# Hybrid decoder layer, down projection of the MLP: one 1024-column VectorE add per product in place of two 512-column sums shared with ScalarE and GpSimd, a new order of the products, and a smaller GpSimd share in the MLP

## The chip, the core and the metric

One core of one Trainium2 chip runs the whole layer. The metric is the device time of one execution in microseconds; three runs of the kernel before give a median of 2394.18 us (2391.11 to 2404.26). Engines are named as in the profile: PE (TensorE matmul), PEld (its weight loads), DVE (VectorE), ACT (ScalarE), POOL (GpSimd), SP (the engine that issues the DMAs).

## The reference

A decoder layer on 2048 tokens of width 1024: a mixer (two groups of gated linear attention heads) and an MLP, each between two RMSNorms. The change lies in the MLP, and almost all of it in the second product:

```python
h = x + rmsnorm(hybrid_mixer(rmsnorm(x, pre_mix_norm), ...), post_mix_norm)
u = jnp.square(jax.nn.relu(rmsnorm(h, pre_mlp_norm) @ w_up))   # 2048x1024 @ 1024x4096
out = h + rmsnorm(u @ w_down, post_mlp_norm)                   # 2048x4096 @ 4096x1024
```

All is float32, and the kernel keeps float32 accuracy.

## The kernel before

The layer runs as three stages one after the other: the mixer (matmuls on lines 232 to 234), `up` (962 to 964) and `down` (1192 to 1194). In this kernel each float32 operand of a matmul is split into a high part of type fp32r and a rest of the same type, `hi` and `lo`, and a product takes three matmuls: hi by hi, hi by lo, lo by hi. The split is `parts()`: ACT copies `raw` to `hi` (L859), and then a subtraction `lo = raw - hi` goes through `tt()`, which gives it to POOL (L850) or DVE (L853). `tt()` keeps a running load for both engines and takes POOL while POOL's sum plus 1.36 is below DVE's plus 0.85. A second layer `_x`, computed without these splits, stands behind a condition and is not executed; all names here end in `_f`.

The MLP's matmuls use a form of Strassen's scheme (Winograd's): a block of 2 x 2 needs seven products, numbered 0 to 6, in place of eight, and sums and differences around them. In `down`, `w_down` is taken in 8 blocks of 512 rows (`kb`). A block has four granules `n` (`GRAN`: 256 tokens of each half block of tokens), and each granule seven products of 12 matmuls: 336 matmuls in a block, 2688 in all. Product `i` of granule `n` reads `u[n, i]` (the activations, combined in `up`, stored in DRAM as `u_operands`, tiles `raw_f` and `u_f`) and `wd[kb][i]` (split weights in the tiles `act_f`). The weights come as four DMAs of 512 KB into the tiles `wr_f` (`down_weights`, L1049); their four differences (tiles `t_f` and `wr_f`) and 14 splits of 512 columns are done in the seven steps ahead of the block's first product and on into its first granule. A step is one product.

Each product adds into one of three PSUM banks, by token half `x`: X holds products 0 and 1, Y 5, 6 and 3, Z 4 and 2, accumulating one on the other. After each product its bank is added into an SBUF tile `acc_f`, and the next product on that bank must wait until the bank is read (and the first of the next granule until a buffer is free: 3 X, 3 Y, 2 Z, each 128 x 512). Those sums are of two kinds:

- `grow()`: DVE adds the bank directly, `acc += bank` (L1131);
- `later()`, for products 5 and 6: ACT copies the bank to a tile `y_f` (L1157), then POOL adds `acc += y` (L1135).

In the first block ACT copies the bank into `acc_f` instead. In the last block the sums of products 5 and 6 also take the sum `a` of product 0 along (DVE `y = bank + acc a`, then an addition by `tt`), and `c21 += a` is a further `tt`. Each finished quarter is squared on ACT with a row sum (L1172) and multiplied with the gain `post` by `tt`; when both halves of a row are there, `finish()` forms the reciprocal root (L239 on DVE, the power L241 on POOL), applies it and adds the residual (L1263 on DVE) and stores the rows (L1266). The residual rows are loaded at L1168, on SP's queue, like the `u` inputs of `down_input` (L1093; one product per DMA, issued seven steps ahead, split five steps ahead).

The order in the program is set by the list `todo` of `down`, sorted by step; on top of it a scheduler reorders the finished program statically for each engine, so the same code elsewhere in the layer can come out in a slightly different order when tiles change.

Of the kernel before, what the change touches and what calls it, by code (L numbers as in the profile page):

```python
# [96 lines left out]
class Layer:  # L97
# [72 lines left out]
    def aslot(self):  # L170
        return self.ac.tile([P, TB], F32R, tag="act", name=self.name("act"), bufs=32)
# [194 lines left out]
    def prepare(self, b, ahead=1):  # L366
# [149 lines left out]
    def tile_task(self, u, i, q, k, g, scale):  # L516
# [31 lines left out]
        for h, og in outs:  # L548
# [4 lines left out]
            self.oT[n] = self.split(self.aslot(), self.aslot(), tr, self.normw[:, n:n + 1])  # L553
# [283 lines left out]
    def left(self, s, i, raws, out, slot):  # L837

        for j in range(4):
# [3 lines left out]
            out.append(self.parts(slot, raw))  # L843

    def tt(self, out, a, b, op):

        nc = self.nc
        if self.load[1] + 1.36 < self.load[0] + 0.85:
            self.load[1] += 1.36
            nc.gpsimd.tensor_tensor(out, a, b, op)  # L850
        else:
            self.load[0] += 0.85
            nc.vector.tensor_tensor(out, a, b, op)  # L853

    def parts(self, new, raw, shape=None):
        hi, lo = new(), new()
        if shape is not None:
            hi, lo = (z.rearrange("p (k n) -> p k n", k=shape) for z in (hi, lo))
        self.nc.scalar.activation(hi, raw, AF.Copy)  # L859
        self.tt(lo, raw, hi.bitcast(F32), ALU.subtract)  # L860
# [15 lines left out]
    def up(self):  # L876
# [3 lines left out]
        with ExitStack() as ctx:  # L880
# [13 lines left out]
            def slot():  # L894


                return self.aslot() if self.place else new("a", 24, F32R)

            def left(s, i):
# [4 lines left out]
                for _ in self.left(s, i, lambda: new("raw", 3), ops[s, i], slot):  # L904
                    pass

            def right(n):
# [11 lines left out]
                part = lambda z: self.parts(lambda: new("w", 12, F32R), z, 4)  # L919
# [121 lines left out]
            self.first_down(lambda: new("wr", 4, F32, 1024), lambda: new("t", 5), lambda: new("raw", 3))  # L1041

    def down_weights(self, kb, wide, temp):
# [3 lines left out]
        for f, h in ((0, 0), (0, 1), (1, 1), (1, 0)):  # L1047
            r = wide().rearrange("p (k n) -> p k n", k=2)
            self.nc.sync.dma_start(r, view[f][:, :, h * 512:h * 512 + 512])  # L1049
            raw.append([r[:, k, :] for k in range(2)])  # L1050
        b11, b12, b22, b21 = raw
        ks = range(2)
        w = self.wd[kb] = {}

        def keep(i, z):
            w[i] = [self.parts(self.aslot, z[k]) for k in ks]

        def diff(out, x, y):
# [19 lines left out]
        keep(4, t1)  # L1078
# [3 lines left out]
        keep(2, b22)  # L1082
        yield


    GRAN = tuple((s, q) for s in range(2) for q in range(2))

    def down_input(self, n, i, raws, slot):

        kb, (s, q) = n // 4, self.GRAN[n % 4]  # L1090
        raw = raws()
        view = self.ud[i, s, 2 * kb:2 * kb + 2].rearrange("k p t -> p k t")
        self.nc.sync.dma_start(raw.rearrange("p (k t) -> p k t", k=2), view[:, :, q * 256:q * 256 + 256])  # L1093
        yield
        self.u[n, i] = self.parts(slot, raw)
        yield

    def first_down(self, wide, temp, raws):

        self.wd, self.u = {}, {}  # L1100
        for _ in self.down_weights(0, wide, temp):
            pass
        for i in self.ORDER[:2]:
            for _ in self.down_input(0, i, raws, self.aslot):
                pass

    def down(self):
# [3 lines left out]
        with ExitStack() as ctx:  # L1111
# [9 lines left out]
            def temp():  # L1121
                return new("t", 4)

            nkb = FF // 512
            npair = 8
            acc, rows = {}, {}
            self.load = [0.0, 0.0]

            def dve_add(out, a, b):
                self.load[0] += 0.69  # L1130
                nc.vector.tensor_add(out, a, b)  # L1131

            def pool_add(out, a, b):
                self.load[1] += 1.36
                nc.gpsimd.tensor_add(out, a, b)  # L1135

            def grow(p, key, z, first):

                if first:
                    acc[p, key] = new("acc", 5 * npair)  # L1140
                    nc.scalar.activation(acc[p, key], z, AF.Copy)
                else:
                    dve_add(acc[p, key], acc[p, key], z)

            def later(p, key, z, first, last):


                if first:
                    acc[p, key] = new("acc", 5 * npair)
                    nc.scalar.activation(acc[p, key], z, AF.Copy)  # L1150
                else:
                    y = new("y", 3)
                    if last:
                        dve_add(y, z, acc[p, "a"])
                        self.tt(acc[p, key], acc[p, key], y, ALU.add)
                    else:
                        nc.scalar.activation(y, z, AF.Copy)  # L1157
                        pool_add(acc[p, key], acc[p, key], y)

            def closed(n, p, key):  # L1160
# [3 lines left out]
                t0 = s * TM + m * TB + q * 256 + p % 2 * P  # L1164
                a = acc[p, key]
                if (p, m) not in rows:
                    h1, ss = wide(), new("ssm", 8, F32, 2)
                    nc.sync.dma_start(h1, self.h1d[t0:t0 + P, :])  # L1168
                    rows[p, m] = (h1, ss, {})
                h1, ss, parts = rows[p, m]  # L1170
                parts[half] = a
                nc.scalar.activation(new("y", 3), a, AF.Square, accum_out=ss[:, half:half + 1])  # L1172
                self.tt(a, a, self.post[half], ALU.mult)
                if len(parts) == 2:
                    tails.append(self.finish(t0, h1, ss, parts))

            def product(n, i):

                kb = n // 4
                hi, lo = (z.rearrange("p (k t) -> p k t", k=2) for z in self.u.pop((n, i)))  # L1180
                b = self.BANK[i]
                for x in range(2):
                    p = 2 * (n % 4) + x
                    first = (p, b) not in bank
                    if first:
                        bank[p, b] = ps.tile([P, TB], F32, tag=b, name=self.name(b), bufs=2 if b == "Z" else 3)
                    z = bank[p, b]
                    tok = slice(x * P, x * P + P)
                    mm = nc.tensor.matmul
# [166 lines left out]
```

## Time and profile before

| what | value |
| --- | --- |
| median of three runs | 2394.18 us (2391.11 to 2404.26) |
| profiled execution, its own time | 2393.46 us |
| its span | 2391.2 us |
| mixer | 0 to 1036.3 us |
| up | 1036.3 to 1702.3 us |
| down, eight blocks | 1702.3 to 2374.3 us |
| after the last matmul | 2374.3 to 2391.2 us |

The stages are told apart by the line of the matmuls. The rows quoted below come from the page, from windows (a stretch, its length, the busy time and count of each engine, then the granted TensorE clock, the DMA share and GB/s), from the waits (engine, tile and line, what it waited for: total, times, longest), from groups (line, engine, operation, out<-in, count | busy us, mean ns | idle time just before them, and what ended it), and from the timeline (start, duration, instruction, [idle before <- what ended it]).

### The profile page before, as it was taken

How to read it: one execution, taken by the hardware profiler on the slowest of the kernel's cores; microseconds unless marked ns; L12 is line 12 of the kernel's file. 1: busy time of each engine (PE TensorE's matmuls, PEld its weight loads, DVE VectorE, ACT ScalarE, POOL GpSimd, SP SyncE). 2: the span in 40 equal slices, each digit the busy share in tenths (PEclk: the TensorE clock that was granted, in tenths of full speed). 3: DMA queues.
4: the chain of work that ended last, by engine and by line, in shares of the span. 5: the costliest groups of instructions: out<-in, count | busy, mean ns of one | idle time of the engine just before them, and what ended most of it. 6: DMA issues, size and time to landing. Idle time of an engine off the chain costs nothing. (4 is left out here: it accounts for less than half of the span.)

```text
span 2391.2 us, 32759 instructions
## 1 busy us (share of the span) xinstructions
PE 2271.7 (95%) x10922; PEld 1852.0 (77%) x10922; DVE 1499.0 (63%) x2492; ACT 1245.3 (52%) x2547; POOL 1156.1 (48%) x855
## 2 busy tenths in 40 slices
PE   7999999999999989979999999999799999999994
PEld 6788878888887878767788878888687777877873
DVE  4675566656755487475545665545556677677698
ACT  5754566456655656455545564554563444334441
POOL 4320323133312542057655665555455677567686
PEclk9999999999999999999999999999899999999997
DMA  6421642256215932278644564444433333333355
GB/s 181 122 79 61 198 133 71 89 147 189 72 57 178 280 113 76 97 240 269 218 153 146 188 214 151 148 146 154 155 110 124 123 123 113 113 119 120 119 169 189
DMA packets 294915, 343.49 MB, mean 144 GB/s; under 512 B 25792, under 2 KB 214480, under 8 KB 294736
## 3 DMA queue, kind: packets, MB, share of 16 engines
q1 hardware_dynamic: 294736, 341.30, 44.8%
q8 instruction: 88, 1.44, 0.2%
q14 instruction: 91, 0.75, 0.1%
HBM read 242.65 MB, written 98.57 MB: 143 GB/s over the span
## 5 line engine op out<-in xcount | busy, mean ns | idle before, releaser
L223 POOL TENSOR_TENSOR w_f<-wr_f,w_f 128x512 fp32r<-128x512 f32 (+1 forms) x160 | 218.8, 1379 | 264.9 <-ACT w_f L222 240.3
L232 PE MATMUL zp_f<-w_f,act_f 128*128 128x512 f32 (+2 forms) x896 | 331.5, 371 | 0.5 <-ACT w_f L222 0.5
L233 PE MATMUL zp_f<-w_f,act_f 128*128 128x512 f32 (+2 forms) x896 | 327.6, 366 | 1.3 <-POOL w_f L223 1.0
L234 PE MATMUL zp_f<-w_f,act_f 128*128 128x512 f32 (+2 forms) x896 | 326.0, 366 | 0.0
L241 POOL TENSOR_TENSOR rs_f<-ms_f,c_neghalf 128x1 f32<-128x1 f32 (+1 forms) x96 | 77.2, 812 | 426.8 <-DVE ms_f L239 426.3
L859 ACT ACTIVATE u_f<-raw_f 128x512 fp32r<-128x512 f32 x222 | 139.4, 630 | 249.7 <-DMA raw_f<-u_operands 65.2
L222 ACT ACTIVATE w_f<-wr_f 128x512 fp32r<-128x512 f32 (+1 forms) x288 | 178.5, 630 | 142.9 <-DMA wr_f<-in_w_in 64.0
L850 POOL TENSOR_TENSOR u_f<-raw_f,u_f 128x512 fp32r<-128x512 f32 x116 | 167.0, 1445 | 99.7 <-ACT u_f L859 80.5
L232 PEld LDWEIGHTS zp_f<-w_f,act_f 128*128 128x128 f32 x896 | 169.4, 189 | 29.9 <-issue 2.2
L233 PEld LDWEIGHTS zp_f<-w_f,act_f 128*128 128x128 f32 x896 | 169.7, 190 | 29.2 <-POOL w_f L223 1.2
L234 PEld LDWEIGHTS zp_f<-w_f,act_f 128*128 128x128 f32 x896 | 169.6, 189 | 27.4 <-issue 0.2
L1135 POOL TENSOR_TENSOR acc_f<-acc_f,y_f 128x512 f32<-128x512 f32 x96 | 141.9, 1482 | 83.8 <-ACT y_f L1157 83.6
L1192 PE MATMUL Y_f<-act_f,u_f 128*128 128x512 f32 x380 | 151.8, 400 | 22.7 <-DVE y_f L1131 13.1
L232 PE MATMUL zp_f<-act_f,w_f 128*128 128x512 f32 x384 | 154.6, 406 | 2.7 <-ACT act_f L222 2.7
L233 PE MATMUL zp_f<-act_f,w_f 128*128 128x512 f32 x384 | 154.7, 403 | 2.1 <-DVE act_f L223 2.1
L853 DVE TENSOR_TENSOR u_f<-raw_f,u_f 128x512 fp32r<-128x512 f32 x106 | 105.1, 992 | 78.8 <-ACT u_f L859 78.8
L234 PE MATMUL zp_f<-act_f,w_f 128*128 128x512 f32 x384 | 153.3, 399 | 0.0
L1193 PE MATMUL Y_f<-act_f,u_f 128*128 128x512 f32 x380 | 150.8, 397 | 0.0
L1194 PE MATMUL Y_f<-act_f,u_f 128*128 128x512 f32 x380 | 149.4, 395 | 0.0
L223 DVE TENSOR_TENSOR w_f<-wr_f,w_f 128x512 fp32r<-128x512 f32 (+1 forms) x128 | 97.7, 775 | 79.0 <-ACT w_f L222 76.7
L859 ACT ACTIVATE w_f<-t_f 128x512 fp32r<-128x512 f32 x128 | 80.0, 628 | 114.8 <-PE Y_f L963 61.4
L850 POOL TENSOR_TENSOR ev_f<-ev_f,ev_f 128x512 f32<-128x512 f32 x67 | 101.5, 1515 | 64.0 <-ACT ev_f L981 63.7
(247 smaller groups left out, 6214.4 us busy)
## 6 DMA issues: line engine op xcount, KB each, us to landing
u_operands<-ev_f SPq DMA_DIRECT2D x224, 256.0 KB, 2.1
raw_f<-u_operands SPq DMA_DIRECT2D x224, 256.0 KB, 2.7
wr_f<-in_w_in SPq DMA_DIRECT2D x256, 128.0 KB, 2.6
wr_f<-in_w_up SPq DMA_DIRECT2D x64, 512.0 KB, 3.7
wr_f<-in_w_in SPq DMA_DIRECT2D x96, 256.0 KB, 3.1
wide_f<-in_x SPq DMA_DIRECT2D x32, 512.0 KB, 6.0
wr_f<-in_w_out SPq DMA_DIRECT2D x64, 256.0 KB, 3.0
wr_f<-in_w_down SPq DMA_DIRECT2D x32, 512.0 KB, 3.7
```

Source lines behind the costliest of these rows:

```text
L222: nc.scalar.activation(hi, raw, AF.Copy)
L223: eng.tensor_sub(lo, raw, hi.bitcast(F32))
L232: mm(out, a[0], b[0], start=i == 0, stop=False)
L233: mm(out, a[0], b[1], start=False, stop=False)
L234: mm(out, a[1], b[0], start=False, stop=i == n - 1)
L850: nc.gpsimd.tensor_tensor(out, a, b, op)
L853: nc.vector.tensor_tensor(out, a, b, op)
L859: self.nc.scalar.activation(hi, raw, AF.Copy)
L1135: nc.gpsimd.tensor_add(out, a, b)
L1192: mm(z, hi[:, k, tok], whi, start=first and k == 0, stop=False, skip_group_check=not first)
L1193: mm(z, hi[:, k, tok], wlo, start=False, stop=False, skip_group_check=not first)
L1194: mm(z, lo[:, k, tok], whi, start=False, stop=k == 1, skip_group_check=not first)
```

## The change

- `down`: every sum after a product is one DVE add of 1024 columns, both token halves at once, directly from PSUM (L1145); only for the last granule's products 2 and 3 it is split in two. There are no copies to `y_f` and no sums on POOL. The banks become tiles of 128 x 1024: X 1, Y 2, Z 1.
- The products' order in `down` is 0, 4, 5, 1, 6, 2, 3 in place of 0, 5, 1, 6, 4, 3, 2. In the last block ACT writes `a` into Y's bank ahead of product 5 (four times, 1024 columns), in place of the extra additions of `a`.
- Inputs of two products are handled together: two DMAs, one copy and one subtraction of 1024 columns; loaded eight steps ahead and split four ahead. The weights' splits and differences are of 1024 columns too (7 and 4 a block); the differences are formed in the `wr_f` tiles themselves.
- `tt()` takes POOL only while POOL's load is below `share` times DVE's; `share` is 0.5, in the last block 1.0 for three granules and 0.5 for the last. This holds in `up` as well.
- The `act_f` tiles are allocated in pairs (also in the mixer and in `up`). `post` is loaded as one tile and scaled by the root of 1024, `finish()` uses one DVE operation ahead of the power in place of two.

```diff
-        if self.load[1] + 1.36 < self.load[0] + 0.85:
-            self.load[1] += 1.36
+        dve, pool = 0.2 + n / 960, 0.1 + n / 400
+        if self.load[1] + pool < self.share * (self.load[0] + dve):
+            self.load[1] += pool
             nc.gpsimd.tensor_tensor(out, a, b, op)
...
+    DOWN = (0, 4, 5, 1, 6, 2, 3)
...
         def keep(i, z):
-            w[i] = [self.parts(self.aslot, z[k]) for k in ks]
+            hi, lo = self.parts(self.along(), self.along(), z, 1024)
+            w[i] = [(hi[:, k * 512:k * 512 + 512], lo[:, k * 512:k * 512 + 512]) for k in range(2)]
...
-        self.u[n, i] = self.parts(slot, raw)
+        hi, lo = self.parts(*pair(), raw, 1024)
+        for x in range(2):
+            self.u[self.seq[m + x]] = [z[:, x * 512:x * 512 + 512].rearrange("p (k t) -> p k t", k=2)
+                                       for z in (hi, lo)]
...
-                        nc.scalar.activation(y, z, AF.Copy)
-                        pool_add(acc[p, key], acc[p, key], y)
...
+                a = acc[p, key]
+                for x in ((slice(0, 512), slice(512, 1024)) if split else (slice(0, 1024),)):
+                    self.load[0] += 1.25
+                    nc.vector.tensor_add(a[:, x], a[:, x], z[:, x])
...
-                        bank[p, b] = ps.tile([P, TB], F32, tag=b, name=self.name(b), bufs=2 if b == "Z" else 3)
+                    bank[n, b] = ps.tile([P, 2 * TB], F32, tag=b, name=self.name(b), bufs=2 if b == "Y" else 1)
...
+                if end and i == 5:
+                    nc.scalar.activation(z, acc[n % 4, "a"], AF.Copy)
+                    loaded = True
...
-                        todo.append((at - 7, 0, "load", n, i))
-                        todo.append((at - 5, 1, "input", n, i))
+                    todo.append((m - 8, 0, "load", m))
+                    todo.append((m - 4, 1, "input", m))
...
-        nc.vector.tensor_add(tot, ss[:, 0:1], ss[:, 1:2])
-        r = self.rstd(tot, D, 1)
+        nc.vector.tensor_scalar(tot, ss[:, 0:1], ss[:, 1:2], D * EPS, ALU.add, ALU.add)
+        r = self.t([P, 1], "rs", bufs=8)
+        nc.gpsimd.tensor_tensor(r, tot, self.c["neghalf"][:, :1], ALU.pow)
```

Two places show how the instructions come to stand. The first is a change of weights: while the last granule of block 4 and the first of block 5 are multiplied, the weights of block 5 are prepared. DVE's queue there, before (L853 on `act_f`, `t_f`, `wr_f` is weight work, L853 on `u_f` the inputs, L1131 the sums from the banks):

```order
L853 TENSOR_TENSOR act_f_19797<-t_f_19792,act_f_19796 128x512
L1131 TENSOR_TENSOR acc_f_16978<-acc_f_16978,X_f_19740 128x512
L1131 TENSOR_TENSOR acc_f_16934<-acc_f_16934,Y_f_19610 128x512
L1131 TENSOR_TENSOR acc_f_16837<-acc_f_16837,Z_f_19670 128x512
L1131 TENSOR_TENSOR acc_f_16846<-acc_f_16846,Z_f_19678 128x512
L853 TENSOR_TENSOR t_f_19793<-wr_f_19576,t_f_19793 128x512
L853 TENSOR_TENSOR act_f_19825<-wr_f_19576,act_f_19824 128x512
L853 TENSOR_TENSOR u_f_19789<-raw_f_19726,u_f_19788 128x512
L853 TENSOR_TENSOR act_f_19829<-wr_f_19576,act_f_19828 128x512
```

and DVE's queue at the same change of weights now:

```order
L1145 TENSOR_TENSOR acc_f_16729<-acc_f_16729,X_f_18777 128x1024
L1145 TENSOR_TENSOR acc_f_16756<-acc_f_16756,Z_f_18803 128x1024
L861 TENSOR_TENSOR wr_f_18654<-wr_f_18658,wr_f_18654 128x1024
L1145 TENSOR_TENSOR acc_f_16714<-acc_f_16714,Y_f_18697 128x1024
L1145 TENSOR_TENSOR acc_f_16776<-acc_f_16776,Y_f_18822 128x1024
L861 TENSOR_TENSOR u_f_18840<-raw_f_18757,u_f_18839 128x1024
L861 TENSOR_TENSOR act_f_18862<-wr_f_18660,act_f_18861 128x1024
L1145 TENSOR_TENSOR acc_f_16802<-acc_f_16802,X_f_18777 128x1024
L861 TENSOR_TENSOR wr_f_18654<-wr_f_18660,wr_f_18654 128x1024
L861 TENSOR_TENSOR act_f_18887<-wr_f_18656,act_f_18886 128x1024
```

A 1024-column sum of every product (Y included) stands between the subtractions, one or two of them at a time. POOL's queue at this place, before:

```order
L850 TENSOR_TENSOR u_f_19709<-raw_f_19664,u_f_19708 128x512
L850 TENSOR_TENSOR t_f_19792<-wr_f_19576,t_f_19792 128x512
L850 TENSOR_TENSOR act_f_19801<-t_f_19793,act_f_19800 128x512
L850 TENSOR_TENSOR u_f_19729<-raw_f_19686,u_f_19728 128x512
L850 TENSOR_TENSOR u_f_19751<-raw_f_19706,u_f_19750 128x512
L1135 TENSOR_TENSOR acc_f_17005<-acc_f_17005,y_f_19773 128x512
L1135 TENSOR_TENSOR acc_f_17014<-acc_f_17014,y_f_19783 128x512
```

and POOL's queue there now:

```order
L858 TENSOR_TENSOR u_f_18728<-raw_f_18647,u_f_18727 128x1024
L858 TENSOR_TENSOR act_f_18818<-wr_f_18654,act_f_18817 128x1024
L858 TENSOR_TENSOR u_f_18795<-raw_f_18724,u_f_18794 128x1024
L858 TENSOR_TENSOR act_f_18844<-wr_f_18654,act_f_18843 128x1024
L858 TENSOR_TENSOR u_f_18882<-raw_f_18791,u_f_18881 128x1024
```

POOL keeps some of the subtractions, now of 1024 columns, and none of the sums. The second place is the last block, DVE's queue before:

```order
L1131 TENSOR_TENSOR acc_f_16822<-acc_f_16822,X_f_21810 128x512
L853 TENSOR_TENSOR acc_f_16726<-acc_f_16726,y_f_21669 128x512
L1131 TENSOR_TENSOR acc_f_16718<-acc_f_16718,Z_f_21678 128x512
L853 TENSOR_TENSOR u_f_21737<-raw_f_21672,u_f_21736 128x512
L1131 TENSOR_TENSOR acc_f_16726<-acc_f_16726,Z_f_21692 128x512
L1131 TENSOR_TENSOR acc_f_16762<-acc_f_16762,Y_f_21596 128x512
L853 TENSOR_TENSOR acc_f_16718<-acc_f_16718,t_f_21355 128x512
```

and DVE's queue in the last block now (L1241 is the former L1263):

```order
L1145 TENSOR_TENSOR acc_f_16511<-acc_f_16511,Y_f_20181 128x1024
L1241 SCALAR_TENSOR_TENSOR acc_f_16369<-acc_f_16369,rs_f_20132,wr_f_20057 128x512
L1241 SCALAR_TENSOR_TENSOR acc_f_16459<-acc_f_16459,rs_f_20132,wr_f_20057 128x512
L1145 TENSOR_TENSOR acc_f_16532<-acc_f_16532,X_f_20142 128x1024
L1241 SCALAR_TENSOR_TENSOR acc_f_16369<-acc_f_16369,rs_f_20138,wr_f_20063 128x512
L1241 SCALAR_TENSOR_TENSOR acc_f_16459<-acc_f_16459,rs_f_20138,wr_f_20063 128x512
L1145 TENSOR_TENSOR acc_f_16511<-acc_f_16511,Z_f_20167 128x1024
L1145 TENSOR_TENSOR acc_f_16496<-acc_f_16496,Y_f_20181 128x1024
L861 TENSOR_TENSOR u_f_20257<-raw_f_20156,u_f_20256 128x1024
```

The additions of `y_f` are gone; sums from the banks and the closing operations are what is left, with an input's subtraction between. The order of a granule's products on PE comes out as 0, 4, the previous granule's 3, then 5, 1, 2, 6.

More of the change, by code (lines that the diff above doesn't have):

```diff
@@ L116, in __init__ @@
         self.load = [0.0, 0.0]
+        self.share = 0.5
         self.tasks = []
@@ L835, in combine, with left @@
             yield
-    def left(self, s, i, raws, out, slot):
+    def left(self, s, i, raws, out, pair):
         for j in range(4):
@@ L903, in left @@
                 self.place = self.ORDER.index(i) < 4
-                for _ in self.left(s, i, lambda: new("raw", 3), ops[s, i], slot):
+                for _ in self.left(s, i, lambda: new("raw", 3), ops[s, i], pair):
                     pass
@@ L918, in right @@
                 w = sets[n] = {}
-                part = lambda z: self.parts(lambda: new("w", 12, F32R), z, 4)
+                part = lambda z: self.parts(
+                    *(new("w", 12, F32R).rearrange("p (k n) -> p k n", k=4) for _ in range(2)), z)
                 def t():
@@ L1119, in wide @@
                 return new("wr", 4, F32, D)
-            def temp():
-                return new("t", 4)
             nkb = FF // 512
-            npair = 8
-            acc, rows = {}, {}
+            acc, rows, bank, tails = {}, {}, {}, []
             self.load = [0.0, 0.0]
[L1129 to L1135, printed above, removed]
@@ L1162, in closed @@
+            def closed(n, key):
                 m, half = {"c11": (0, 0), "c12": (0, 1), "c22": (1, 1), "c21": (1, 0)}[key]
                 s, q = self.GRAN[n % 4]
-                t0 = s * TM + m * TB + q * 256 + p % 2 * P
+                p = n % 4
                 a = acc[p, key]
[L1166 to L1175, printed above, removed]
+                for x in range(2):
+                    t0 = s * TM + m * TB + q * 256 + x * P
+                    if (p, m, x) not in rows:
+                        h1, ss = wide(), new("ssm", 8, F32, 2)
+                        nc.sync.dma_start(h1, self.h1d[t0:t0 + P, :])
+                        rows[p, m, x] = (h1, ss, {})
+                    h1, ss, parts = rows[p, m, x]
+                    parts[half] = a[:, x * 512:x * 512 + 512]
+                    nc.scalar.activation(new("y", 2), parts[half], AF.Square, accum_out=ss[:, half:half + 1])
+                    self.tt(parts[half], parts[half], self.post[:, half * 512:half * 512 + 512], ALU.mult)
+                    if len(parts) == 2:
+                        tails.append(self.finish(t0, h1, ss, parts))
@@ L1212, in product @@
[L1212 to L1225 removed]
+                        mm(zx, hi[:, k, tok], whi, start=not loaded and k == 0, stop=False, skip_group_check=loaded)
@@ L1226, in down @@
                 if n % 4 == 0 and n:
-                    todo.append((7 * n - 14, 2, "weights", n // 4, None))
+                    if i == self.DOWN[0]:
+                        todo.append((m - 14, 2, "weights", m))
+                    todo.append((m - 6, 2, "weights", m))
             todo.sort(key=lambda x: x[:2])
-            bank, gens, tails = {}, {}, []
-            for _, _, what, n, i in todo:
+            gens = {}
+            for _, _, what, m in todo:
+                n, i = self.seq[m]
@@ L1231, in down @@
                 if what == "step":
-                    if i == self.ORDER[0]:
-                        bank.clear()
+                    if i == self.DOWN[0] and n >= 4 * nkb - 4:
+                        self.load, self.share = [0.0, 0.0], 1.0 if n < 4 * nkb - 1 else 0.5
+                        if n == 4 * nkb - 4:
+                            self.post = new("post", 1, F32, D)
+                            nc.sync.dma_start(self.post, io["post_mlp_norm"].broadcast_to([P, D]))
+                            nc.scalar.activation(self.post, self.post, AF.Copy, scale=float(D) ** 0.5)
```

176 lines of the change are left out of this document (70 added, 106 removed).

## The prediction

> **What bounds the kernel now.** I read the page's busy shares first, then windows of each stage and block, then the waits of PE in each, and last the timeline where those waits lie.
>
> ```profile
> PE 2271.7 (95%) x10922; PEld 1852.0 (77%) x10922; DVE 1499.0 (63%) x2492; ACT 1245.3 (52%) x2547; POOL 1156.1 (48%) x855
> ```
>
> PE carries the time, but the average hides where it stands still. The windows (length, then busy time of PE, PEld, DVE, ACT, POOL; clock) of `up`, of blocks 0 to 7 of `down` (the second row is an undisturbed piece of block 0), and of the stretch after the last matmul:
>
> ```profile
> 1111.30:1690.00 578.70, 569.49 (x2455) 461.43 (x2453) 326.86 (x397) 310.14 (x521) 338.39 (x241) 1.00 0.50 170
> 1717.30:1790.00 72.70, 72.70 (x322) 60.18 (x321) 36.60 (x41) 45.28 (x82) 37.37 (x26) 1.00 0.42 137
> 1702.30:1785.30 83.00, 78.62 (x337) 64.59 (x336) 36.71 (x42) 46.72 (x84) 37.71 (x28) 0.96 0.49 162
> 1785.30:1863.80 78.50, 76.52 (x338) 63.01 (x338) 55.96 (x68) 34.62 (x61) 51.39 (x36) 1.00 0.38 121
> 1863.80:1944.20 80.40, 78.03 (x337) 64.13 (x336) 55.86 (x69) 33.91 (x59) 54.69 (x39) 0.98 0.37 118
> 1944.20:2024.20 80.00, 77.01 (x337) 62.82 (x336) 58.50 (x69) 33.62 (x58) 55.59 (x40) 1.00 0.37 116
> 2024.20:2104.60 80.40, 77.05 (x337) 62.86 (x337) 56.27 (x69) 33.76 (x59) 55.59 (x38) 1.00 0.38 118
> 2104.60:2189.00 84.40, 78.63 (x337) 63.98 (x336) 58.39 (x70) 33.84 (x59) 54.73 (x39) 0.98 0.37 113
> 2189.00:2270.70 81.70, 78.64 (x338) 63.98 (x337) 58.04 (x68) 33.76 (x59) 56.14 (x39) 0.98 0.39 122
> 2270.70:2374.30 103.60, 84.74 (x338) 66.78 (x336) 100.10 (x141) 34.30 (x83) 79.79 (x59) 0.92 0.56 183
> 2374.30:2391.20 16.90, 0.03 (x1) 0.00 (x0) 10.76 (x20) 2.06 (x6) 6.28 (x7) 0.65 0.40 150
> 2102.00:2118.00 16.00, 11.77 (x50) 8.75 (x48) 16.00 (x14) 6.44 (x11) 15.02 (x10) 1.00 0.22 67
> ```
>
> PE's pace is 72.70/322 = 0.226 us a matmul, so a block of 336 can't take less than 75.9 us, a product of 12 takes 2.72 and a granule 19.04. Against that floor block 0 loses 7.1, blocks 1 to 6 lose 2.6, 4.5, 4.1, 4.5, 8.5 and 5.8 (30.0 together), and block 7 loses 27.7. After the last matmul 16.9 us remain. In block 7 DVE is busy 100.10 of 103.60 us, and in the last row, 16 us at the change to block 5's weights, DVE is busy all the time. PE's waits (total, times, longest; the first two from blocks 1 to 6, the next two from block 7, then `up` and the start of `down`):
>
> ```profile
> PE Z_f L1192 <- DVE acc_f L1131: 10.0, 7, 2.5
> PE Y_f L1192 <- DVE acc_f L1131: 9.3, 5, 2.7
> PE Y_f L1192 <- DVE y_f L1131: 13.1, 3, 6.3
> PE Z_f L1192 <- DVE ms_f L239: 3.5, 1, 3.5
> PE Y_f L962 <- DVE ev_f L977: 14.5, 4, 7.9
> PE X_f L1192 <- ACT u_f L859: 4.4, 1, 4.4
> ```
>
> So what ends last is DVE reading a bank. Why DVE is late stands in the timeline of both engines at the same change of weights:
>
> ```profile
> 2101.60 1.75 POOL L1135 TENSOR_TENSOR acc_f<-acc_f,y_f 128x512 f32<-128x512 f32 x1
> 2102.12 1.77 DVE L853 TENSOR_TENSOR u_f<-raw_f,u_f 128x512 fp32r<-128x512 f32 x1
> 2103.82 1.78 DVE L853 TENSOR_TENSOR wr_f<-wr_f,wr_f 128x512 f32<-128x512 f32 x1
> 2107.22 0.67 DVE L1131 TENSOR_TENSOR acc_f<-acc_f,X_f 128x512 f32<-128x512 f32 x1
> 2118.71 1.27 DVE L1131 TENSOR_TENSOR acc_f<-acc_f,Z_f 128x512 f32<-128x512 f32 x2
> 2122.31 0.68 DVE L853 TENSOR_TENSOR u_f<-raw_f,u_f 128x512 fp32r<-128x512 f32 x1
> 2125.12 1.29 POOL L1135 TENSOR_TENSOR acc_f<-acc_f,y_f 128x512 f32<-128x512 f32 x1 [6.88 <-ACT y_f L1157]
> ```
>
> A DVE subtraction of two SBUF tiles takes 0.68 us while POOL rests (2122.31) and 1.77 beside a POOL operation: the one at 2102.12 ends 0.54 us after POOL's ends at 2103.35, as if it began only then. POOL's addition grows likewise from 1.29 to 1.75. The sum from PSUM takes 0.67 in the midst of it: not held. So subtractions wait for whole POOL instructions, and the sums queue behind them.
>
> **The change part by part.** Durations first. Two 512 sums in a row take 1.27; a row count of one column, L239 below, takes 0.143, so a column costs (0.68 - 0.14)/512 = 1.05 ns and 1024 columns 1.22 us, or 1.14 at the pitch of such operations in a row (0.60 for 512, from 1.27 less 0.67). Bounds: 0.68 (width is free) and 1.27 (width saves nothing). For POOL I take 2 x 1.25 = 2.5 for 1024, the price with nothing saved, its bound above; below lies 1.29.
>
> ```profile
> L853 DVE TENSOR_TENSOR u_f<-raw_f,u_f 128x512 fp32r<-128x512 f32 x106 | 105.1, 992 | 78.8 <-ACT u_f L859 78.8
> L1131 DVE TENSOR_TENSOR acc_f<-acc_f,Z_f 128x512 f32<-128x512 f32 x128 | 86.3, 680 | 69.7 <-POOL acc_f L1135 38.1 <-PE Z_f L1194 25.3 <-ACT u_f L859 4.3
> L1135 POOL TENSOR_TENSOR acc_f<-acc_f,y_f 128x512 f32<-128x512 f32 x96 | 141.9, 1482 | 83.8 <-ACT y_f L1157 83.6
> L1263 DVE SCALAR_TENSOR_TENSOR acc_f<-acc_f,rs_f,wr_f 128x512 f32<-128x512 f32 x32 | 35.3, 1149 | 0.8 <-POOL rs_f L241 0.7
> L859 ACT ACTIVATE u_f<-raw_f 128x512 fp32r<-128x512 f32 x222 | 139.4, 630 | 249.7 <-DMA raw_f<-u_operands 65.2 <-PE Y_f L1193 63.2 <-PE X_f L1193 53.3
> L239 DVE TENSOR_SCALAR ms_f<-ss_f 128x1 f32<-128x1 f32 x16 | 2.0, 143 | 0.0
> L241 POOL TENSOR_TENSOR rs_f<-ms_f,c_neghalf 128x1 f32<-128x1 f32 x16 | 12.6, 790 | 6.9 <-DVE ms_f L239 6.9
> ```
>
> *Changes of weights (six).* Gone are POOL's 96 sums (141.9 us), ACT's 96 copies, and DVE's 38.1 us of waiting for those sums. Added to DVE are the sums of products 5 and 6. In the granule ahead of a block DVE now has 7 sums and, by the counts of the changed program, some 8.5 weight operations and 1.75 of inputs, 10 in all, of 1024 columns: 17 x 1.14 = 19.4 us. POOL has some 4.5 of 2.5 us. A DVE subtraction that starts inside one of these waits it out; I let half of them hit, since POOL is busy 11.2 of 19 us: 19.4 + 2.25 x 2.5 = 25.0. Against it stand 19.04 us of PE and a slack: in PE's new order each bank rests two other products, 5.44 us, before it is used again, less 1.22 for the sum: 4.2, together 23.3. The stall is 1.7 per change, 10 for six where 30.0 were lost: **-20**. Bounds: no hits, no stall, -30; all 4.5 hit, 30.7, stall 7.4 less some tenths that overlap, 42 in all, +12.
>
> The Trainium skill has this as a rule ("SBUF — State Buffer", section "Who interferes with whom"): DVE and GpSimd share one pair of SBUF ports that is locked for a whole instruction, a DVE operation with two SBUF inputs contends with a GpSimd one that reads SBUF, and the loser blocks fully. The rows at 2101.60 and 2102.12 agree. It speaks against this change in one respect: instructions twice as long hold the lock twice as long. By it a hit costs 2.5 and the sum stands; if a hit cost the 1.1 seen at 512 columns, the changes of weights would stall nothing and the sum come 10 us lower.
>
> *Last block.* Per granule DVE has 7 sums (8.0), 8 of the L1263 kind (4.8 at the pitch of 0.60), 1.75 multiplications with `post` (1.0), 1.25 input subtractions (1.4) and small ones (0.4): 15.6 us. The extra sums of `a` are gone from DVE; their four replacements on ACT (1024 columns, at most 2 x 0.63 each) hide under ACT's 34.30 busy of 103.60. POOL has 6.25 multiplications of 1.25 and 1.75 subtractions of 2.5: 12.2 us. With half of it held against DVE: 21.7 against 19.04, 2.7 x 4 = 11, less the slack of 4.2 once, plus the slow restart of PE. That restart shows in the row below: after 3.68 us of standing still the next matmuls stand 0.43 apart instead of 0.226, for some eight of them, 1.6 us; I count three. The loss becomes 12 instead of 27.7: **-16**. Bounds: no loss, -28; all held, 8.8 x 4 = 35, +7.
>
> ```profile
> 2311.47 0.80 PE L1192 MATMUL Y_f<-act_f,u_f 128*128 128x512 f32 x1 [3.68 <-DVE y_f L1131]
> 2312.06 0.63 PE L1193 MATMUL Y_f<-act_f,u_f 128*128 128x512 f32 x1
> 2312.49 0.63 PE L1194 MATMUL Y_f<-act_f,u_f 128*128 128x512 f32 x1
> 2311.80 7.59 DMA raw_f<-u_operands
> 2384.43 1.41 DVE L1263 SCALAR_TENSOR_TENSOR acc_f<-acc_f,rs_f,wr_f 128x512 f32<-128x512 f32 x2 [0.66 <-POOL rs_f L241]
> ```
>
> *After the last matmul.* The last DVE operation ends at 2385.84, so 5.4 us of the 16.9 are the output's DMA, which stays. The rest becomes: half a sum 0.67, square 0.63, a multiplication on POOL 1.29, the power 0.79, four of L1263 at 0.68 to 1.15, handovers: 7.3 to 9.2. I take 14 for 16.9: **-3** (-4.2 to 0).
>
> *Start of `down`.* The first input is now two products in one piece, one copy longer by 0.6 and one subtraction longer by 0.54 ahead of the first matmul, which waited 4.4 for it: **+1** (0 to +3). Later pairs have a lead of four products, 10.9 us, for at most 1.27 on ACT and 2.5 on POOL: hidden. The DMAs are as many, on the same queue, a step earlier: 0.
>
> *`up`.* PE waits 14.5 us in four places for DVE to empty Y. By the counts the subtractions move from POOL (268 to 143) to DVE (310 to 385). POOL operations that can hold DVE fall by 47 %, and I let the waits fall by as much: **-6**. Bounds: all 14.5 go; or DVE's 75 more, 51 us, cut its idle time from 252 to 201 and the waits grow in that ratio to 18.2: -14.5 to +4.
>
> *Mixer.* Only the tiles' pairing and the scheduler's order change: 0, with 5 either way for waits that fall elsewhere.
>
> The sum is -20 - 16 - 3 + 1 - 6 = -44 on the profiled execution of 2393.46, which lies 0.7 below the median: **2350**.
>
> **The rivals.** *A, slower.* DVE is the new bound, held by long POOL operations: with the ends above (+12, +7, and -2 for the rest) 2410. The gain at a change of weights is gone when the stall reaches the 5.0 of now, so from (28.3 - 19.4)/2.5 = 3.6 hits of 4.5. Against it: a sum from PSUM isn't held, and POOL's 15.02 of 16 us there falls to 11. Held about halfway between, all stays near 2388: no change. *B, the last block stays as it is.* SP issues the inputs' loads behind stores that wait for DVE's closing operations (L1263), and the chain that ended last goes through that queue to the input's DMA of 7.59 us at 2311.80. The change leaves that order on SP: if it sets the last block's pace as the sums get out of its way, 2350 + 16 = 2366. Against it speak 16.6 us of PE's waits there with DVE's name, and 4.4 with an input's, at the start of `down`. *C, every stall of `down` goes* (no hits matter): -30 - 28 - 3 + 1 - 6 = 2328.
>
> **How the numbers follow.** The forecast 2350 gets 0.50, B 0.17, C 0.13, no change 0.13, A 0.07. A measurement of this kernel tells apart 0.5 %, 12 us. The first three are faster by more, 0.80. The range from 2323 to 2385 holds those three and little of the last two, which is 0.2 left out.
>
> **What would show it.** Right: sums at L1145 of 1.1 to 1.27 us, never longer; PE's waits for DVE at the changes of weights under 12 us in all; blocks 1 to 6 at 76 to 78.5 us; the last block at 84 to 92, with DVE busy under 90 %; PE's wait for `ev_f` in `up` nearer 8. Wrong: sums of 1024 columns that cost over 1.3 us, or 1024-column subtractions on DVE of 3 us or more at most changes of weights (A), or a last block over 100 us whose PE waits name `u_f` (B).

## Result and the profile after

The changed kernel takes 2339.96 us (median of four runs, 2337.40 to 2341.28) against 2393.11 (median of four): a ratio of 0.976, 95 % interval 0.974 to 0.979. The profiled execution is the fastest of the four, 2337.40 us with a span of 2335.5, so the differences below are some 2.5 us larger than those of the medians. By stage, each from its first matmul to the next one's (us):

| stage | before | after | difference | forecast |
| --- | --- | --- | --- | --- |
| mixer | 1036.3 | 1034.0 | -2.4 | 0 |
| up | 666.2 | 655.0 | -11.3 | -6 |
| down, block 0 | 83.0 | 80.7 | -2.3 | +1 |
| blocks 1 to 6 | 485.3 | 459.5 | -25.9 | -20 |
| block 7 | 103.4 | 92.3 | -11.1 | -16 |
| after the last matmul | 16.9 | 14.1 | -2.8 | -3 |

The page's busy shares, then the windows of `up`, of blocks 0, 1, 2, 6 and 7 and of the end (PE, PEld, DVE, ACT, POOL):

```profile
PE 2256.8 (97%) x10922; PEld 1844.5 (79%) x10922; DVE 1507.8 (65%) x2368; ACT 1170.8 (50%) x2268; POOL 778.1 (33%) x537
```

```profile
1111.30:1678.00 566.70, 563.11 (x2434) 456.39 (x2432) 373.72 (x486) 307.25 (x507) 199.49 (x136) 1.00 0.50 173
...
1688.90:1769.63 80.73, 79.07 (x336) 63.98 (x337) 32.77 (x28) 42.79 (x44) 16.57 (x7) 0.98 0.52 169
1769.63:1845.79 76.16, 76.16 (x337) 63.03 (x336) 53.07 (x41) 22.78 (x22) 28.54 (x11) 1.00 0.35 112
1845.79:1924.28 78.49, 76.52 (x338) 62.91 (x336) 58.66 (x43) 21.85 (x21) 26.48 (x11) 1.00 0.39 130
...
2152.93:2229.09 76.16, 76.16 (x337) 63.06 (x336) 53.27 (x43) 21.97 (x21) 27.27 (x12) 1.00 0.39 127
2229.09:2321.43 92.34, 82.41 (x337) 65.63 (x335) 79.01 (x80) 35.75 (x76) 60.63 (x44) 0.94 0.62 205
2321.43:2335.50 14.07, 0.00 (x0) 0.00 (x0) 8.72 (x12) 1.33 (x4) 5.90 (x6) 0.59 0.42 155
```

In blocks 1 and 6 PE is busy for the whole of 76.16 us: that is a block's floor, and 3, 4 and 5 stand at it too (76.2 to 76.3). Block 2 loses 2.3 us: PE waits 2.0 there for a copy of ACT. POOL's work has fallen from 1156 to 778 us while DVE's has stayed (1499 to 1508). PE's waits in the whole kernel that bear on the change:

```profile
PE Y_f L1186 <- DVE acc_f L1145: 9.0, 3, 3.9
...
PE X_f L968 <- ACT ev_f L1005: 5.3, 1, 5.3
PE Y_f L968 <- DVE ev_f L983: 4.2, 3, 2.7
PE Z_f L968 <- DVE ev_f L983: 3.8, 1, 3.8
...
PE X_f L1186 <- DVE ev_f L983: 2.5, 1, 2.5
PE X_f L1186 <- ACT act_f L864: 2.0, 1, 2.0
```

All of the 9.0 lies in block 7. At the changes of weights no wait of PE for DVE is left. Holding is not gone, though. DVE at the change into block 5, and POOL beside it:

```profile
2065.96 1.22 DVE L1145 TENSOR_TENSOR acc_f<-acc_f,Y_f 128x1024 f32<-128x1024 f32 x1 [1.27 <-PE Y_f L1188]
2067.10 3.14 DVE L861 TENSOR_TENSOR u_f<-raw_f,u_f 128x1024 fp32r<-128x1024 f32 x1
```

```profile
2064.38 2.42 POOL L858 TENSOR_TENSOR u_f<-raw_f,u_f 128x1024 fp32r<-128x1024 f32 x1 [3.05 <-ACT u_f L864]
2066.75 2.42 POOL L858 TENSOR_TENSOR act_f<-wr_f,act_f 128x1024 fp32r<-128x1024 f32 x1
```

The sum takes 1.22 us beside a POOL operation; the subtraction takes 3.14, as it ends 1.07 us after POOL's ends at 2069.17. That is the price of a hit at 1024 columns. The longest subtraction of blocks 0 to 6 takes 3.42; the five of 3 us or more lie at three of the six changes, and none of them stalls PE.

### The profile page after: what moved, and what is told of

The parts are those of the page before. It is cut to its first block, busy times and chain, and to the rows that moved or that the text cites. A ratio compares the mean times of both kernels' runs of the same rounds, so it can differ in the third digit from the quotient of the medians.

```text
span 2335.5 us, 31584 instructions
## 1 busy us (share of the span) xinstructions
PE 2256.8 (97%) x10922; PEld 1844.5 (79%) x10922; DVE 1507.8 (65%) x2368; ACT 1170.8 (50%) x2268; POOL 778.1 (33%) x537
## 5 line engine op out<-in xcount | busy, mean ns | idle before, releaser
L864 ACT ACTIVATE u_f<-raw_f 128x1024 fp32r<-128x1024 f32 x111 | 117.7, 1061 | 330.5 <-PE Y_f L1187 219.1
L858 POOL TENSOR_TENSOR u_f<-raw_f,u_f 128x1024 fp32r<-128x1024 f32 x55 | 135.4, 2462 | 302.0 <-ACT u_f L864 301.8
L247 POOL TENSOR_TENSOR rs_f<-ms_f,c_neghalf 128x1 f32<-128x1 f32 (+1 forms) x80 | 65.1, 823 | 450.2 <-DVE ms_f L245 440.7
L1145 DVE TENSOR_TENSOR acc_f<-acc_f,Y_f 128x1024 f32<-128x1024 f32 (+1 forms) x89 | 107.1, 1204 | 67.0 <-PE Y_f L1188 65.9
L861 DVE TENSOR_TENSOR w_f<-t_f,w_f 128x512 fp32r<-128x512 f32 x98 | 86.1, 878 | 48.2 <-ACT w_f L864 48.2
L858 POOL TENSOR_TENSOR ev_f<-ev_f,ev_f 128x512 f32<-128x512 f32 x40 | 63.8, 1594 | 141.8 <-ACT ev_f L987 79.2
```

Of the source, the lines that this page charges most:

```text
L1145: nc.vector.tensor_add(a[:, x], a[:, x], z[:, x])
```

## The experiments

All of them in one table: stage times as above, and the ratio to the kernel before with its 95 % interval.

| kernel | up | block 0 | 1 to 6 | block 7 | end | median | ratio |
| --- | --- | --- | --- | --- | --- | --- | --- |
| b_up_share | 654.6 | 83.5 | 483.8 | 104.8 | 16.9 | 2382.2 | 0.996 (0.993 to 0.999) |
| b_sums_dve | 667.0 | 83.2 | 461.7 | 106.8 | 14.5 | 2373.1 | 0.992 (0.990 to 0.994) |
| b_order | 664.5 | 84.6 | 486.4 | 104.1 | 19.9 | 2399.7 | 1.002 (1.001 to 1.004) |
| b_three | 653.3 | 83.6 | 462.5 | 94.7 | 15.0 | 2350.9 | 0.981 (0.979 to 0.982) |
| a_share_old | 668.1 | 84.5 | 458.5 | 92.8 | 14.5 | 2353.6 | 0.983 (0.981 to 0.985) |
| a_order1 | 653.9 | 86.2 | 457.9 | 90.0 | 14.8 | 2342.7 | 0.978 (0.976 to 0.981) |
| a_pool0 | 657.4 | 82.1 | 457.2 | 94.8 | 14.5 | 2342.0 | 0.977 (0.975 to 0.980) |
| a_sum512 | 657.0 | 82.5 | 465.2 | 90.4 | 20.9 | 2352.6 | 0.981 (0.978 to 0.983) |
| a_extra | 654.4 | 80.9 | 459.6 | 96.2 | 21.5 | 2349.1 | 0.981 (0.978 to 0.984) |
| a_last_half | 656.3 | 82.5 | 459.5 | 83.4 | 20.9 | 2339.3 | 0.976 (0.973 to 0.979) |
| a_last_short | 654.9 | 80.7 | 459.6 | 86.0 | 21.4 | 2340.2 | 0.975 (0.973 to 0.977) |
| a_up_quarter | 653.2 | 82.6 | 459.5 | 93.3 | 14.1 | 2342.0 | 0.976 (0.974 to 0.979) |

Those named b_ start from the kernel before, those named a_ from the changed one.

### `up`: the share alone

```diff
...
+        dve, pool = (0.73, 1.38) if self.share < 1 else (0.85, 1.36)   # share 0.5 in up, 1.0 in down
+        if self.load[1] + pool < self.share * (self.load[0] + dve):
...
```

> The kernel before, with the new rule for the split between POOL and DVE (share 0.5) in `up` alone; `down` keeps the old rule. Theory (POOL's subtractions hold DVE's, and DVE empties the banks late): `up` gets about the 11 us shorter that it got in the changed kernel (666 to 655 us), the rest stays; about 2382 us, ratio 0.995. Rival (the gain in `up` came from the paired tiles or the scheduler's order): `up` stays at 666 us, 2393 us.

`up` fell by 11.6 us, and no other stage moved by more than 2.5. The reverse, in the changed kernel:

```diff
-        self.share = 0.5
+        self.share = 1.0
...
-        dve, pool = 0.2 + n / 960, 0.1 + n / 400
+        dve, pool = 0.85 * n / 512, 1.36 * n / 512
...
```

> The changed kernel with the old rule for the split (POOL at 1.36 against DVE at 0.85 per 512 columns, share 1). Theory: POOL's operations hold DVE again; `up` gets 11 us longer, and stalls of 2 to 4 us come back at each of the six changes of weights (12 to 24 us together); about 2368 us. Rival (the smaller share of POOL does nothing, the sums and the order do it all): 2340 us.

`up` grew by 13.1 us (in an execution 4.9 above the median of its four), and the changes of weights by nothing: the half of the expectation on them failed. The run also sets the share of the last granule to 1.0. The wait of PE for DVE in `up`, of b_up_share and of a_share_old:

```profile
PE Y_f L964 <- DVE ev_f L979: 9.0, 3, 5.1
```

```profile
PE Y_f L968 <- DVE ev_f L983: 12.2, 5, 4.7
```

Before it was 14.5. Taken both ways, the share accounts for all of the gain in `up`. Less still:

```diff
-        self.share = 0.5
+        self.share = 0.25        # in up; down 0.5 as before
```

> The changed kernel with POOL's share at 0.25 instead of 0.5 in `up`, `down` as it is. Theory (POOL's subtractions hold DVE, which empties the banks): `up` has 655 us and its matmuls' pace allows about 645, so a further 3 to 5 us go; 2336 us. Rival (DVE gets too full: 374 us busy of 567 would become about 420): `up` grows again, 660 us or more, 2345 us.

`up` took 653.2 us, 1.8 less, and the kernel's time did not change: neither expectation was met, and 0.5 is enough.

### Blocks 1 to 6: sums, order, share

```diff
                     else:
-                        nc.scalar.activation(y, z, AF.Copy)
-                        pool_add(acc[p, key], acc[p, key], y)
+                        dve_add(acc[p, key], acc[p, key], z)
```

> The kernel before, with the sums of products 5 and 6 added by DVE straight from PSUM in blocks 1 to 6 (512 columns each), nothing else. Theory: POOL loses 96 sums, but the running load then hands it more subtractions, which hold DVE as before, and the banks rest as short as before; the 30 us lost in blocks 1 to 6 fall to about 20, the last block stays; about 2384 us. Rival (the detour over ACT and POOL, with DVE's 38 us of waiting for it, is the loss): under 8 us are left in blocks 1 to 6, 2370 us.

The rival was right on the size: 461.7 us, 4.8 above the floor of 6 x 76.16. Its reason is another matter. The order alone:

```diff
...
-                for j, i in enumerate(self.ORDER):
+                for j, i in enumerate(self.DOWN):        # 0, 4, 5, 1, 6, 2, 3; weights prepared in that order
...
```

> The kernel before, with the new order of the products in `down` (0, 4, 5, 1, 6, 2, 3) alone; sums, widths and the split between POOL and DVE as before. Theory: a bank rests two other products instead of one (4.2 us of slack for the sums instead of 1.5), so that the loss of blocks 1 to 6 falls from 30 to about 15 us and that of the last block from 28 to about 20; about 2371 us. Rival (DVE is full there, so that slack only moves the wait): 2390 us.

No gain at all. But it tells more. In the kernel before DVE waited 38.1 us for POOL's sums; with the new order that wait is gone, and the loss is the same. The group of Z's sums in blocks 0 to 6 of b_order, whose idle time now has PE's name:

```profile
L1133 DVE TENSOR_TENSOR acc_f<-acc_f,Z_f 128x512 f32<-128x512 f32 x103 | 70.0, 683 | 46.8 <-PE Z_f L1196 46.7
```

So to be rid of that wait gained nothing by itself. The trace of the kernel before says the same: ahead of each of PE's eleven waits for a sum of over 0.3 us in its blocks 1 to 6, DVE had worked without a gap for 8 us or more. In those last 8 us its subtractions took 3.8 to 5.5 us longer together than at 0.68 each, every time more than the wait of 0.6 to 2.7. What this looks like stands in the timeline of b_order at the change into block 5 (POOL, DVE and PE, in three fences):

```profile
2110.44 1.74 POOL L850 TENSOR_TENSOR u_f<-raw_f,u_f 128x512 fp32r<-128x512 f32 x1
2112.14 1.72 POOL L850 TENSOR_TENSOR act_f<-t_f,act_f 128x512 fp32r<-128x512 f32 x1
2113.93 1.59 POOL L850 TENSOR_TENSOR t_f<-wr_f,t_f 128x512 f32<-128x512 f32 x1
```

```profile
2110.95 1.78 DVE L853 TENSOR_TENSOR act_f<-wr_f,act_f 128x512 fp32r<-128x512 f32 x1
2112.65 1.75 DVE L853 TENSOR_TENSOR wr_f<-wr_f,wr_f 128x512 f32<-128x512 f32 x1
2114.33 1.75 DVE L853 TENSOR_TENSOR u_f<-raw_f,u_f 128x512 fp32r<-128x512 f32 x1
2116.00 0.68 DVE L1133 TENSOR_TENSOR acc_f<-acc_f,Z_f 128x512 f32<-128x512 f32 x1
```

```profile
2116.73 0.50 PE L1194 MATMUL Z_f<-act_f,u_f 128*128 128x512 f32 x1 [3.72 <-DVE acc_f L1133]
```

Three subtractions, each held to 1.75 us or more by a POOL operation, stand ahead of the sum; each alternates with POOL's next one. Then two kernels that take this apart from both sides:

```diff
-            self.load = [0.0, 0.0]
+            self.load, self.share = [0.0, 0.0], 0.0      # blocks 0 to 6: every subtraction on DVE
```

> The changed kernel with none of the subtractions of blocks 0 to 6 of `down` on POOL, all on DVE (the last block as it is). Theory of the prediction: nothing is held, but the granule ahead of a block then holds 24.5 us of DVE work against 23.3 of room: 1.2 us per change, 2347 us. Rival (DVE's work can spread further than that granule): blocks 1 to 6 stay at 458 to 460 us, 2340 us.

```diff
-    DOWN = (0, 4, 5, 1, 6, 2, 3)
+    DOWN = (0, 4, 1, 5, 2, 6, 3)                         # weights prepared in that order
...
```

> The changed kernel with the products in the order 0, 4, 1, 5, 2, 6, 3, in which X's and Y's banks rest mostly one other product (2.7 us) instead of two. Theory of the prediction (the slack of 4.2 us is what takes up the held subtractions): stalls come back at the changes of weights, 10 us or more in blocks 1 to 6; about 2352 us. Rival (after the sums have left POOL, nothing there needs the slack): blocks 1 to 6 stay under 463 us, 2340 us.

Both went the rival's way: 457.2 and 457.9 us. The groups of DVE's weight subtractions in blocks 0 to 6 show the holding itself (mean ns of one): of the changed kernel, of a_share_old, and of a_pool0.

```profile
L861 DVE TENSOR_TENSOR act_f<-wr_f,act_f 128x1024 fp32r<-128x1024 f32 x37 | 62.6, 1691 | 8.8 <-ACT act_f L864 6.5 <-PE Z_f L1188 2.2
```

```profile
L861 DVE TENSOR_TENSOR act_f<-wr_f,act_f 128x1024 fp32r<-128x1024 f32 x23 | 48.8, 2122 | 8.3 <-ACT act_f L864 8.3
```

```profile
L861 DVE TENSOR_TENSOR act_f<-wr_f,act_f 128x1024 fp32r<-128x1024 f32 x47 | 57.3, 1220 | 4.6 <-PE Z_f L1188 2.2 <-ACT act_f L864 2.1
```

With POOL empty every subtraction takes 1.22 us. Adding up, over blocks 0 to 6, DVE's subtractions of two SBUF tiles less 0.68 (512 columns) or 1.22 us (1024) for each gives the time held:

| kernel | DVE's subtractions | busy us | held us | POOL busy us | loss, blocks 1 to 6 |
| --- | --- | --- | --- | --- | --- |
| before | 195 of 512 | 227.8 | 95.2 | 365.8 | 28.4 |
| b_order | 203 of 512 | 227.9 | 89.9 | 368.0 | 29.4 |
| b_sums_dve | 107 of 512 | 125.4 | 52.6 | 345.0 | 4.8 |
| b_three | 107 of 512 | 125.9 | 53.1 | 342.8 | 5.6 |
| a_share_old | 57 of 1024 | 112.8 | 43.3 | 298.2 | 1.4 |
| a_sum512 | 75 of 1024 | 131.8 | 40.3 | 252.2 | 8.1 |
| after | 109 of 1024 | 164.1 | 31.1 | 168.1 | 2.5 |
| a_order1 | 108 of 1024 | 155.0 | 23.2 | 165.2 | 1.0 |
| a_pool0 | 175 of 1024 | 213.5 | 0.0 | 1.3 | 0.0 |

Held time of 90 us and more goes with a loss of 28 to 29, 53 with 5 to 6; below that the order is lost (40.3 with 8.1, 43.3 with 1.4). Moving sums to DVE was a trade: the running load gave POOL 88 subtractions in their place, so that DVE's queue had sums, which are not held, instead of subtractions, which are. POOL stayed nearly as busy. A second reading fits as well: the moved sums leave the contest between the two engines altogether. POOL's time and DVE's subtractions at 0.68 or 1.22 us each add to 498 us in the kernel before, 418 in b_sums_dve and 301 in the changed kernel. No run tells these two apart. With the sums of 1024 columns on DVE, the split of the subtractions mattered little: 57, 108, 109 or all 175 of them on DVE lost 1.4, 1.0, 2.5 and 0.0 us. That subtractions held by POOL make the sums late is shown by the timelines; that the held time alone sets the loss is not shown, since the nine kernels differ in other things too. POOL kept for the sums alone, with all subtractions on DVE, was not run.

### Width of the sums

```diff
-                grow(n, key, z, n == 4 * nkb - 1 and i in (2, 3))
+                grow(n, key, z, True)                    # two additions of 512 columns
```

> The changed kernel with every sum after a product in two DVE additions of 512 columns instead of one of 1024. Theory (what counted was that DVE reads the bank itself; two additions of 0.60 us cost 0.06 more than one of 1.14): blocks 1 to 6 stay at 458 to 461 us and the whole at 2340 us. Rival (fewer and wider instructions are part of the gain): blocks 1 to 6 grow by 6 us or more.

By the ratios some 10 us slower than the changed kernel, but the edit did more than it should: each half is booked in the running load at the price of the whole, so POOL got more subtractions (252.2 us of work in place of 168.1). Of the 8.1 us lost in blocks 1 to 6, 6 are one wait of 3.55 us in block 5 and PE's slow restart. The experiment is inconclusive on width. The last kernel below, all of 512 columns, bounds what the width can be worth.

### The last block

```diff
-                if end and i == 5:
-                    nc.scalar.activation(z, acc[n % 4, "a"], AF.Copy)
-                    loaded = True
+                if end and i in (5, 6, 3):               # behind grow()
+                    self.tt(acc[n % 4, key], acc[n % 4, key], acc[n % 4, "a"], ALU.add, 1024)
```

> The changed kernel without the write of `a` into Y's bank in the last block; instead `a` is added in SBUF to the sums of products 5, 6 and 3 (12 additions of 1024 columns, shared between DVE and POOL). Theory (the last block's loss is the work on the port that DVE and POOL share): 12 x 1.14 us on DVE or 12 x 2.4 on POOL come back, the last block grows from 92 to about 99 us; 2347 us. Rival (the last block's gain came from the direct sums and the wider instructions): it stays at 92 us, 2340 us.

The theory held on the size, at another place than it said: block 7 grew by 3.9 us and the end by 7.4, 11.3 together. What holds up block 7 of the changed kernel at the worst place, DVE, POOL and PE:

```profile
2274.43 7.02 DVE L1241 SCALAR_TENSOR_TENSOR acc_f<-acc_f,rs_f,wr_f 128x512 f32<-128x512 f32 x4 [0.44 <-POOL rs_f L1237]
2281.37 1.21 DVE L1145 TENSOR_TENSOR acc_f<-acc_f,Y_f 128x1024 f32<-128x1024 f32 x1
2283.43 0.21 DVE L1235 TENSOR_SCALAR ss_f<-ssm_f 128x1 f32<-128x1 f32 x1 [0.85 <-ACT y_f L1161]
2284.04 0.21 DVE L1235 TENSOR_SCALAR ss_f<-ssm_f 128x1 f32<-128x1 f32 x1 [0.40 <-ACT y_f L1161]
2284.17 1.21 DVE L1145 TENSOR_TENSOR acc_f<-acc_f,Y_f 128x1024 f32<-128x1024 f32 x1
```

```profile
2274.88 5.36 POOL L858 TENSOR_TENSOR u_f<-raw_f,u_f 128x1024 fp32r<-128x1024 f32 x2
```

```profile
2285.44 0.50 PE L1186 MATMUL Y_f<-act_f,u_f 128*128 128x512 f32 x1 [3.94 <-DVE acc_f L1145]
```

Four closing operations, 2.4 us at 0.60 each, take 7.02 beside two long subtractions on POOL, and Y's sums are late. The sum at 2281.37 isn't yet the one that PE waits for: it finishes a quarter, which ACT then squares, and DVE's queue stands still 0.85 and 0.40 us for these squares ahead of two one-column additions (L1235). Only behind them comes the sum at 2284.17, whose end at 2285.38 lets PE go on. The second of the three waits, 1.76 us at 2309.10, ends behind the same two additions. A queue with the sum ahead of them was not run. Two attempts to shorten the held closings:

```diff
-                        self.load, self.share = [0.0, 0.0], 1.0 if n < 4 * nkb - 1 else 0.5
+                        self.load, self.share = [0.0, 0.0], 0.5
```

> The changed kernel with POOL's share at 0.5 in all four granules of the last block (1.0 in three of them now). Theory: an instruction costs the shared port about twice as long on POOL as on DVE, so less on POOL shortens the 7 us for which four closing operations of DVE stood beside two subtractions on POOL; the last block falls from 92 to about 86 us; 2334 us. Rival (DVE is the fuller engine there): it grows to 95 us or more, 2343 us.

```diff
-        if self.load[1] + pool < self.share * (self.load[0] + dve):
+        if self.load[1] + pool < self.share * (self.load[0] + dve) and not (n > 512 and self.short):   # block 7
...
```

> The changed kernel with the 1024-column input subtractions of the last block all on DVE; POOL keeps the multiplications of 512 columns there, at the shares of the change. Theory (long POOL operations hold the closing operations of DVE, 7.0 us for four at the worst place): the last block falls from 92 to about 86 us, while the stretch after the last matmul stays near 14 us, because POOL still takes its multiplications; 2333 us. Rival (DVE's own work sets the end, and each piece moved to it comes back later, as with the share of 0.5): last block and end together stay at 104 to 107 us, 2339 us.

Both did what their theories said in block 7 (83.4 and 86.0 us in place of 92.3) and gave it back afterwards: the end took 20.9 and 21.4 instead of 14.1, so that the times forecast, 2334 and 2333, were missed; for the second kernel the rival had said so. The end of a_last_half, PE's last matmul and what DVE still has to do:

```profile
2316.64 0.39 PE L1188 MATMUL Y_f<-act_f,u_f 128*128 128x512 f32 x1
```

```profile
2316.19 3.43 DVE L861 TENSOR_TENSOR acc_f<-acc_f,post_f 128x512 f32<-128x512 f32 x2
2319.54 1.40 DVE L1241 SCALAR_TENSOR_TENSOR acc_f<-acc_f,rs_f,wr_f 128x512 f32<-128x512 f32 x2
2320.87 1.27 DVE L1145 TENSOR_TENSOR acc_f<-acc_f,Z_f 128x512 f32<-128x512 f32 x2
2322.07 1.27 DVE L1145 TENSOR_TENSOR acc_f<-acc_f,Y_f 128x512 f32<-128x512 f32 x2
...
2325.92 6.38 DVE L1241 SCALAR_TENSOR_TENSOR acc_f<-acc_f,rs_f,wr_f 128x512 f32<-128x512 f32 x8 [1.30 <-POOL rs_f L1237]
```

PE is done at 2317.0, but the last sums wait until 2320.87 behind multiplications and closings. From the start of block 7 to the end of the kernel it takes 106.4 us in the changed kernel, 104.3 and 107.4 in these two, and DVE is busy for 87.7, 91.3 and 89.9 of them. The likeliest reading is that DVE's queue, with what it is held, sets the end, and not PE; no run isolates it. Neither version's time can be told from the changed kernel's, and no other run beat it.

### Three parts together

```diff
+        dve, pool = (0.73, 1.38) if self.share < 1 else (0.85, 1.36)   # share 0.5 in up, 1.0 in down
...
-                        nc.scalar.activation(y, z, AF.Copy)
-                        pool_add(acc[p, key], acc[p, key], y)
+                    dve_add(acc[p, key], acc[p, key], z)               # in block 7 too
...
+                    if kb == nkb - 1 and i == 5:
+                        nc.scalar.activation(z, acc[p, "a"], AF.Copy)
```

> The kernel before with three parts of the change together and all instructions still 512 columns wide, in the old order of the products, with single tiles: POOL's share of 0.5 in `up`, all sums by DVE straight from PSUM, and `a` written into Y's bank by ACT in the last block. Theory (these three are the change): the single results add up, 11.6 us in `up`, 21.5 by the sums (2391.2 to 2369.7 of span), 11.3 in the last block and after it (from the changed kernel without that write): a span of 2347 us, a time of 2349 us; blocks 1 to 6 at 460 to 463. Rival (the wide instructions and the order are what lets the last block gain): last block and end together stay at 117 us or more, 2359 us.

The span was 2348.8 us where the sum of the parts gave 2347, and block 7 and the end together took 109.7, well under the rival's 117. These three make 42.4 of the 55.7 us. What stays for the width, the order, the pairs of tiles and the smaller share in `down` is 13.3 between these two executions (10.5 by the ratios), of which 5.6 lie in the start of `up` (1039.6 against 1034.0), which varies by itself: it came between 1034.0 and 1038.3 in kernels whose mixer is the same.

## Why the prediction was right

The time was inside the range, and the gain larger than the forecast: 53 us by the medians, 55.7 by the spans, against 44. That the time came as near as 10 us to the forecast is in part luck: the last block fell short by 5 us while the changes of weights, `up`, the start and the mixer went 6, 5, 3 and 2 us beyond, and the mixer's length varies by itself (1034.0 to 1038.3 in kernels where it is the same). By its steps:

- **Changes of weights, -20: measured -25.9.** The mechanism (subtractions held for whole POOL instructions, sums queued behind) is borne out by the timelines of the kernel before and of b_order; a_pool0 shows the price without holding, 1.22 us, but starts from a kernel that no longer stalled there. Two terms were wrong. The slack of the new order, 4.2 us, bought nothing: the order alone changed nothing, and a_order1 with less slack lost nothing. And the work was put too tightly: the sum laid 17 DVE operations and 4.5 of POOL into one granule, 25.0 us. In 19 us around five changes the trace has 13 to 17 DVE operations and 2 to 4 of POOL; DVE is busy 18.5 on average and POOL 7.9, and the rest of the work lies before and after. In a_pool0 DVE is busy 18.55 of 19 us at each of these changes, and PE never waits there. So no stall for DVE was left where 1.7 per change was forecast.
- **Last block, -16: measured -11.1.** The place was right: DVE, 79.01 of 92.34 us busy, and 9.0 us of PE's waits. Block 7 loses 16.2 us against 76.16 where the step left 12. PE stands still for 9.9, where the step's sum has 6.8, and its matmuls take 6.2 longer at a granted clock of 0.94, where three slow restarts of 1.6 were counted. The longest wait begins with a hit between POOL's 2.7 us subtractions and a run of closings (7.02 us for four) and ends with DVE's own wait for ACT's squares, which the step has no term for. 11.3 us of block 7 and end together hang on the sums of `a` that are gone.
- **End, -3: measured -2.8. Start, +1: measured -2.3.** The wait of 4.4 us that the step laid ahead of the first matmul stood ahead of the third product, 10 us later (1712.52). There PE now waits 1.0 us, and 3.4 in a_last_half, whose start is the same; kernels with that start have 80.7 to 82.6 us for block 0. So the step read the place wrongly, and the sign isn't settled.
- **`up`, -6: measured -11.3.** All of it is the share, as two kernels show. PE's waits for DVE's `ev_f` fell from 15.4 to 10.5 us, of which 2.5 lie just ahead of `down`'s first matmul; those for POOL's own outputs fell as well, 4.8 to 2.1, while those for ACT's `ev_f` grew from 1.0 to 5.3. In all PE stands still 7.9 us less in `up` (27.2 to 19.3), and its matmuls take 3.4 less (639.1 to 635.6). The step had no term for the matmuls' pace nor for POOL's outputs.
- **Rivals.** A (slower) did not come: sums are not held, 1.20 to 1.22 us throughout. B (the last block as it was) did not come either. C, -66, came nearly true in blocks 1 to 6 alone, where 2.5 us of 28.4 are left.

The Trainium skill's rule on the shared ports ("SBUF — State Buffer", section "Who interferes with whom") agrees with the rows here: DVE's sum from PSUM takes 1.22 us beside POOL and without it, a subtraction of two SBUF tiles 1.22 alone and up to 3.42 beside POOL. Another remark of the Trainium skill in that section, that issue order decides who blocks, fits the alternation in b_order, where each engine's operation takes 1.6 to 1.8 us in place of 1.29 and 0.68.

## What to carry to other kernels

Where operations of two engines hold each other for whole instructions, as the subtractions of DVE and POOL do here, look for work that needn't take part (here a sum read from PSUM) and do it there, in place of a detour over the other engine. Look for the short, urgent operation behind the held ones in the same queue, and price a hit at the other engine's full instruction. Look also for an operation ahead of it that waits for a third engine. How the subtractions were split hardly mattered in blocks 1 to 6 once the sums were on DVE in one piece, but it was worth 11 us in `up`. A gain inside the last block was worth nothing here, since the closing operations gave it back: add up block and end together before counting it.

## Not expected of the hardware

Wide instructions save little on any of the three engines: one of 1024 columns takes 1.22 us on DVE against 1.27 for two of 512 in a row, 2.44 on POOL against twice 1.29, and 1.06 on ACT (a copy) against 1.15 for two in a row. And with the sums on DVE, POOL's load could go from 298 us (a_share_old) to 1 (a_pool0) in seven blocks while the loss of blocks 1 to 6 went only from 1.4 us to 0.0.
